# A mixture-of-experts kernel whose ScalarE and VectorE keep the order of the program in the experts, with two more result buffers and one load buffer fewer

## The chip, the cores and the metric

The kernel runs on one core of a Trainium2 chip. The metric is the time of one execution in device microseconds. A core has five engines that run side by side and wait for each other through semaphores: TensorE (PE, matrix products into the accumulator memory PSUM), VectorE (DVE), ScalarE (ACT), GpSimd (POOL) and SyncE (SP, which issues the loads here). Each engine works through its own queue in order, so an instruction that waits holds all those behind it on that engine.

## The reference

Two layers on 256 tokens of 1,024 channels, all in float32. Each layer has a mixer (dilated attention, stick-breaking attention and a convolution, gated and added). The first layer then has a dense feed-forward block, the second a mixture of eight experts, of which each token takes two:

```python
logits = h @ w_router + b_router
top_logits, top_idx = lax.top_k(logits, 2)
gates = softmax(top_logits)
...
def expert_block(xb, e):
    a = xb @ w_exp_gate[e]
    u = xb @ w_exp_up[e]
    return (silu(a) * u) @ w_exp_down[e]
...
x = x + segment_sum(expert_block(...) * gate, token)
```

Each expert has three matrices of 1,024 x 2,816. They have to be loaded in full, whatever the number of tokens.

## The kernel before, in words

**Products.** A float32 weight is split into a high part `hi` (a rounding copy, by ScalarE) and a low part `lo = weight - hi` (a subtraction, by VectorE); both go through TensorE as its fast 32-bit type. `_Stream` does this for all weights: `_make` (line 265) loads a chunk into a `raw` buffer by SyncE's queue, issues `hi` (line 284) and `lo` (line 288) into `part` buffers, and `next` hands the oldest pair out and calls for further ones, up to `AHEAD_E`, that is three units of 128 x 2,048 beyond the one in use. There are `RAW_BUFS + MORE_BUFS` = 9 `raw` buffers in the experts, and 8 `part` buffers, which hold four pairs. A unit of half the size, both parts in one buffer, is called `hilo`.

**An expert** (`expert`, from line 1155) goes through 22 units of gate and up weights, alternately two for the gate (`eg`) and two for the up projection (`eu`), 512 output columns each; the last two units hold 256 columns of both. Such a group of four I call a round. Twelve units (two of them half) of down weights follow (`ed`, two banks in turn). TensorE's products of a unit are in `products` (line 1168). A long expert has up to 128 rows and takes three products per weight tile (`hi` twice, `lo` once), so 12 matmuls per unit. A short expert (at most 64 rows) puts both parts of the activations side by side in the 128 columns of its left operand, and takes two, 8 per unit; the lower half of the result must then be folded onto the upper, for which ScalarE copies it to `low` (line 1180) and TensorE multiplies that by `fold` (line 1183). ScalarE applies Silu into `ea` (line 1210), VectorE multiplies by `eu` (line 1213), TensorE transposes the product (`eaT`, line 1194), and ScalarE and VectorE split the transposed result into `ehl` in a result buffer (`split_evac`, lines 509 and 510). Result buffers come from the function `T`, which takes `MOE_SLABS` = 8 of them in turn in the experts.

**A seam.** At an expert's end both banks of `ed` are split into `yhi` (ScalarE, line 509) and `ylo` (VectorE, line 510), each half of the columns by itself. `scatter` (line 1134) multiplies them by the permutation `pmt` that puts rows back to their tokens (`sc`, lines 1138 and 1139, two banks for each half), ScalarE copies a bank out, scaled by the gate (`add`, line 1143), and GpSimd adds it to `x` (line 1144). In the last expert VectorE does both at once (line 1146). The program asks for all that while the next expert's first units are already under way: `later(n, f)` runs `f` after `n` further units. Odd experts also gather the rows of the next two (`gather`: `pm`, `xg`). `count` ranks the experts by their number of tokens, in E0, and `ranked` in its result is what SyncE reads to address the loads of the third to the eighth expert.

**Order.** The code is written in one order, and a scheduler of the framework decides in which order each engine's queue gets its instructions, from its own estimate of when each could start. What is wrapped in `keep_in_program_order` (`_InOrder`, and the names `act_`, `dve_`) stays in the order written. In the experts, before the change, ScalarE and VectorE instructions are free. The ranks are worked in the order 0, 1, 5, 2, 6, 3, 4, 7; ranks 5, 6 and 7 are short. I call the eight E0 to E7 in the order of work: E2, E4 and E7 are short.

Of the kernel before, what the change touches and what calls it, by code (L numbers as in the profile page):

```python
# [7 lines left out]
F32 = mybir.dt.float32  # L8
# [4 lines left out]
ALU = mybir.AluOpType  # L13
# [20 lines left out]
RAW_BUFS = 5  # L34
PART_BUFS = 4
SLABS = 17
MORE_BUFS = 4
MORE_PARTS = 4
AHEAD = 3 * 1024
AHEAD_E = 3 * 2048  # L40
WARM = 7
MOE_SLABS = 8
UNIT_E = 2048
SHORT = P // 2

# [164 lines left out]
class _InOrder:  # L210


    def __init__(self, tc, engine):
        self.tc = tc
        self.engine = engine
# [7 lines left out]
class _Stream:  # L223
# [3 lines left out]
    def __init__(self, tc, raw_pool, part_pool, ahead):  # L227
        self.tc = tc
        self.nc = tc.nc
        self.raw_pool = raw_pool  # L230
        self.part_pool = part_pool
        self.ahead = ahead
        self.plan = []
        self.units = []
        self.raws = {}
        self.more_pool = None
        self.more_parts = None
        self.hold = None
        self.lo_late = None
        self.turn = -1  # L240
        self.part_turn = -1
        self.made = 0
        self.waiting = 0

    def raw_tile(self, shape):

        n = RAW_BUFS + (MORE_BUFS if self.more_pool else 0)
        self.turn = (self.turn + 1) % n
        pool = self.raw_pool if self.turn < RAW_BUFS else self.more_pool
        return pool.tile(shape, F32, tag="raw", name="raw")  # L250
# [16 lines left out]
    def _make(self):  # L267
        nc = self.nc
        key, ci, u, ku, n = self.units[self.made]
        size = ku * n  # L270
        self.made += 1
        self.waiting += size
        src, length = self.plan[ci]
        if ci not in self.raws:
            raw = self.raw_tile([P, length])
            nc.sync.dma_start(raw, src() if callable(src) else src)
            self.raws = {ci: raw}
        part = self.raws[ci][:, u * size:(u + 1) * size]
        if 2 * size <= UNIT_E:
            both = self.part_tile("hilo")  # L280
            hi, lo = both[:, :size], both[:, size:2 * size]
        else:
            hi, lo = (self.part_tile(q)[:, :size] for q in ("hi", "lo"))
        ins = nc.scalar.activation(hi, part, AF.Copy)  # L284
        if self.lo_late is not None:
            self.tc.keep_in_program_order(ins)
        if self.lo_late is None:
            nc.vector.tensor_tensor(lo, part, hi.bitcast(F32), op=ALU.subtract)  # L288
        else:
            self.lo_late.append(lambda e: e.tensor_tensor(lo, part, hi.bitcast(F32), op=ALU.subtract))  # L290
        return (key, size, hi.rearrange("p (k n) -> p k n", n=n), lo.rearrange("p (k n) -> p k n", n=n))
# [34 lines left out]
def tile_kernel(ctx, tc, x, weights, experts, columns, consts, gains, out, dbg=None):  # L326
    nc = tc.nc
    dbg = dbg or {}
    pe, act, dve, pool = nc.tensor, nc.scalar, nc.vector, nc.gpsimd

    pe_, act_, dve_, pool_ = (_InOrder(tc, e) for e in (pe, act, dve, pool))
# [5 lines left out]
    small = ctx.enter_context(tc.tile_pool(name="small", bufs=4))  # L337
    slab = ctx.enter_context(tc.tile_pool(name="slab", bufs=MOE_SLABS))
    dense = ExitStack()
    slab2 = dense.enter_context(tc.tile_pool(name="slab2", bufs=SLABS - MOE_SLABS))  # L340
    slabs = {"turn": -1, "of": [slab if i < MOE_SLABS else slab2 for i in range(SLABS)]}
    work = dense.enter_context(tc.tile_pool(name="work", bufs=2))
# [57 lines left out]
    ws = _Stream(tc, raw_pool, part_pool, ahead=AHEAD)  # L400
# [633 lines left out]
        rt["slots"].append(sl)  # L1034

    def moe():
        hhi, hlo, rs2, sels, picks, slots = (rt[k] for k in ("hi", "lo", "rs2", "sels", "picks", "slots"))

        low_1 = lambda e: low(1)
# [289 lines left out]
    def to_moe():  # L1329
# [6 lines left out]
        nc.sync.dma_start(rt["gain"], gains)  # L1336
        ws.more_pool = ctx.enter_context(tc.tile_pool(name="more", bufs=MORE_BUFS))
        ws.more_parts = ctx.enter_context(tc.tile_pool(name="more_parts", bufs=MORE_PARTS))
# [10 lines left out]
    for l in range(L):  # L1349
        mixer(l, *[route] * (l == L - 1))  # L1350
        for t in range(TT):
            dump(f"xm{l}{t}", xs[t])
        if l == 0:
            ffn()
            for t in range(TT):
                dump(f"xf{t}", xs[t])
        else:
            moe()
# [37 lines left out]
```

## Time and profile before

| | |
|---|---|
| median of three runs | 1552.11 us (1551.28 to 1553.24) |
| the profiled execution | 1555.26 us |
| its span (first to last instruction) | 1553.4 us |
| TensorE busy | 1469.4 us, 95%, 6717 matmuls |
| VectorE busy | 1197.7 us, 77%, 1261 instructions |
| ScalarE busy | 1009.9 us, 65%, 1056 instructions |
| GpSimd busy | 101.3 us, 7% |
| read from memory | 397.88 MB, 257 GB/s over the span |
| chain that ended last | TensorE 66%, VectorE 18%, ScalarE 8%, "issue" 5% |

The experts fill the second half of the span, from about 751 us on; the rest are the two mixers and the dense block. The table says that TensorE is busy nearly always, but it is an average over stages, and a busy matmul may still be one that was stretched. Where a stage has room is seen from the busy time of each engine in its own stretch; why, from the chain of waits in it. "Idle before" a group of instructions is the time in which the engine had nothing to do ahead of them, with the instruction that ended it. PEclk, the seventh figure of a stretch, is the clock that TensorE was granted, as a share of the full one.

### The profile page before, as it was taken

To read this page: it belongs to the slowest core of one execution; us is meant where nothing else is said; L and a number is where in the kernel's file an instruction comes from. 1 tells how busy PE (TensorE), PEld (TensorE's weight loads), DVE (VectorE), ACT (ScalarE), POOL (GpSimd) and SP (SyncE) were. 2 spreads that over 40 slices of the span, in tenths; PEclk is the share of its full clock that TensorE was granted. 3 is DMA by queue.
4 is the path that set the end of the run, shared out by engine and by line. 5 is a ranking of instruction groups with operands and counts; after the bars stand their busy time and mean duration, and the time that the engine had idled before them with its cause. 6 is when DMAs were issued, how large, how long until landed. Compare 5 with 4: busy or idle time off the path is not lost.

```text
span 1553.4 us, 18165 instructions
## 1 busy us (share of the span) xinstructions
PE 1469.4 (95%) x6717; PEld 1147.1 (74%) x6717; DVE 1197.7 (77%) x1261; ACT 1009.9 (65%) x1056; POOL 101.3 (7%) x69
## 2 busy tenths in 40 slices
PE   9979999999999989999999999889998899999886
PEld 7867787788888777787888887557775577877554
DVE  6898657555547797666898888888888888888777
ACT  6646653544436556663877778777777767766774
POOL 0200000000000200000000202020020010200200
PEclk9999999999999999999899999999999999999998
DMA  8443345555555343447599989999898898988982
GB/s 350 139 168 128 136 162 174 179 189 173 182 189 188 136 163 111 156 167 284 217 374 374 358 324 364 344 349 349 312 395 337 341 358 323 393 327 319 343 328 104
DMA packets 57696, 400.18 MB, mean 258 GB/s; under 512 B 6528, under 2 KB 6784, under 8 KB 10752
## 3 DMA queue, kind: packets, MB, share of 16 engines
q1 hardware_dynamic: 57312, 398.85, 69.3%
q8 instruction: 54, 0.88, 0.2%
q14 instruction: 42, 0.34, 0.1%
q10 hardware_dynamic: 288, 0.10, 0.0%
HBM read 397.88 MB, written 1.05 MB: 257 GB/s over the span
## 4 chain that ended last, share of the span: by engine, by line
PE 66%; DVE 18%; ACT 8%; issue 5%; POOL 2%; DMA 0%; ACTq 0%; DVEq 0%; SPq 0%
PE ed L1168 11%; PE eg L1168 10%; PE eu L1168 9%; DVE lo L288 8%; ACT hi L284 6%; DVE acc L607 4%; DVE hilo L288 3%; PE gt L449 2%; PE gt L447 2%; PE gt L448 2%; POOL qkss L669 1%; PE fg L448 1%; PE fg L449 1%; PE fg L447 1%; PE fd L447 1%
## 5 line engine op out<-in xcount | busy, mean ns | idle before, releaser
L288 DVE TENSOR_TENSOR lo<-raw,hi 128x2048 fp32r<-128x2048 f32 x253 | 586.9, 2338 | 96.1 <-ACT hi L284 94.6
L284 ACT ACTIVATE hi<-raw 128x2048 fp32r<-128x2048 f32 x253 | 477.0, 1913 | 35.5 <-PE ed L1168 18.6
L288 DVE TENSOR_TENSOR hilo<-raw,hilo 128x1024 fp32r<-128x1024 f32 x244 | 295.1, 1221 | 177.4 <-ACT hilo L284 177.1
L284 ACT ACTIVATE hilo<-raw 128x1024 fp32r<-128x1024 f32 x248 | 257.8, 1058 | 230.5 <-PE fd L449 35.5
L1168 PE MATMUL eg<-hi,xg 128*128 128x512 f32 x608 | 160.8, 400 | 2.5 <-ACT hi L284 2.3
L1168 PE MATMUL eu<-hi,xg 128*128 128x512 f32 x520 | 135.3, 397 | 1.8 <-ACT hi L284 1.8
L1168 PE MATMUL ed<-hi,ehl 128*128 128x512 f32 x516 | 134.4, 397 | 1.4 <-ACT hi L284 1.4
L1168 PEld LDWEIGHTS eg<-hi,xg 128*128 128x128 f32 x608 | 110.9, 188 | 32.5 <-ACT hi L284 8.9
L1168 PE MATMUL eg<-lo,xg 128*128 128x512 f32 x376 | 106.1, 403 | 13.4 <-DVE lo L288 13.4
L1168 PEld LDWEIGHTS eu<-hi,xg 128*128 128x128 f32 x520 | 96.9, 189 | 28.5 <-ACT hi L284 6.1
L1168 PEld LDWEIGHTS ed<-hi,ehl 128*128 128x128 f32 x516 | 95.4, 189 | 25.1 <-ACT hi L284 4.3
L1144 POOL TENSOR_TENSOR x<-x,add 128x512 f32<-128x512 f32 x28 | 69.6, 2513 | 640.7 <-ACT add L1143 640.7
L1168 PE MATMUL eu<-lo,xg 128*128 128x512 f32 x320 | 92.1, 409 | 16.3 <-DVE lo L288 16.2
L1168 PE MATMUL ed<-lo,ehl 128*128 128x512 f32 x316 | 89.8, 406 | 13.4 <-DVE lo L288 12.6
L607 DVE SCALAR_TENSOR_TENSOR acc<-uT,cols,acc 128x255 f32<-128x255 f32 (+29 forms) x240 | 97.1, 462 | 0.0
L1168 PEld LDWEIGHTS eg<-lo,xg 128*128 128x128 f32 x376 | 67.9, 188 | 34.3 <-DVE lo L288 20.4
L1168 PEld LDWEIGHTS eu<-lo,xg 128*128 128x128 f32 x320 | 56.7, 188 | 42.4 <-DVE lo L288 29.6
L1168 PEld LDWEIGHTS ed<-lo,ehl 128*128 128x128 f32 x316 | 57.5, 189 | 35.9 <-DVE lo L288 24.0
L447 PE MATMUL gt<-hilo,hhi 128*128 128x512 f32 x192 | 76.9, 401 | 0.0
L449 PE MATMUL gt<-hilo,hhi 128*128 128x512 f32 x192 | 75.1, 391 | 0.0
L448 PE MATMUL gt<-hilo,hlo 128*128 128x512 f32 x192 | 75.1, 391 | 0.0
L509 ACT ACTIVATE ehl<-eaT 128x512 fp32r<-128x512 f32 (+2 forms) x48 | 23.4, 487 | 71.9 <-PE eaT L1194 61.7
(299 smaller groups left out, 2340.4 us busy)
## 6 DMA issues: line engine op xcount, KB each, us to landing
raw<-in_experts_dram SPq DMA_DIRECT2D x255, 1024.0 KB, 6.7
raw<-in_weights_dram SPq DMA_DIRECT2D x111, 1024.0 KB, 4.8
raw<-in_experts_dram SPq DMA_DIRECT2D x18, 512.0 KB, 4.5
raw<-in_weights_dram SPq DMA_DIRECT2D x4, 512.0 KB, 6.8
x<-in_x_dram SPq DMA_DIRECT2D x2, 512.0 KB, 4.3
out_dram<-x SPq DMA_DIRECT2D x4, 256.0 KB, 2.7
gain<-in_gains_dram SPq DMA_DIRECT2D x1, 512.0 KB, 3.5
att<-in_consts_dram SPq DMA_DIRECT2D x1, 448.0 KB, 7.0
```

What stands on the lines that cost most here:

```text
L284: ins = nc.scalar.activation(hi, part, AF.Copy)
L288: nc.vector.tensor_tensor(lo, part, hi.bitcast(F32), op=ALU.subtract)
L447: pe.matmul(dst, ahi, whi, start=first, stop=False)
L448: pe.matmul(dst, alo, whi, start=False, stop=False)
L449: pe.matmul(dst, ahi, wlo, start=False, stop=last)
L509: act.activation(hi, src, AF.Copy)
L607: dve.scalar_tensor_tensor(acc[:, c, lag:], uT[:, c, :S - lag], w, acc[:, c, lag:], op0=ALU.mult, op1=ALU.add)
L669: pool.tensor_tensor(ssf, ssf, half[:, :TT * 8], op=ALU.pow)
L1144: pool.tensor_tensor(xs[t][:, sl], xs[t][:, sl], add, op=ALU.add)
L1168: pe.matmul(b, lhs(q, k0 + j), w[:, j, :], start=k0 + j == 0 and x == 0, stop=k0 + j == nk - 1 and x == len(todo) - 1)
```

## The change

`moe` now replaces the names `act` and `dve` by the wrapped ones and sets a flag in the stream, so that all ScalarE and VectorE instructions of the experts, `hi` and `lo` among them, stay in the order in which the program issues them. TensorE, GpSimd and SyncE are still ordered by the scheduler. Two more of the 17 result buffers are kept for the experts (`MOE_SLABS` 10), and there is one `raw` buffer fewer (8). In the dense part no instruction of ScalarE or VectorE changes its place.

```diff
-MORE_BUFS = 4
+MORE_BUFS = 3
...
-MOE_SLABS = 8
+MOE_SLABS = 10
...
+        self.in_order = False
...
         ins = nc.scalar.activation(hi, part, AF.Copy)
-        if self.lo_late is not None:
+        if self.lo_late is not None or self.in_order:
             self.tc.keep_in_program_order(ins)
         if self.lo_late is None:
-            nc.vector.tensor_tensor(lo, part, hi.bitcast(F32), op=ALU.subtract)
+            ins = nc.vector.tensor_tensor(lo, part, hi.bitcast(F32), op=ALU.subtract)
+            if self.in_order:
+                self.tc.keep_in_program_order(ins)
...
     def moe():
+        nonlocal act, dve
+        act, dve, ws.in_order = act_, dve_, True
```

Three places show how the orders move. In the changed kernel an instruction that goes through the wrapper has the wrapper's line, L219, and those of `_make` are five lines further down or less.

ScalarE in the middle of the short expert E4, a little over a round (`low_9048` is the copy of the same two units in both), before:

```order
L1180 ACTIVATE low_9048<-eg_9017 64x512
L284 ACTIVATE hi_9022<-raw_9020 128x2048
L1210 ACTIVATE ea_9018<-eg_9017,rss_8725 64x512
L284 ACTIVATE hi_9036<-raw_9034 128x2048
L1180 ACTIVATE low_9088<-eu_9019 64x512
L284 ACTIVATE hi_9054<-raw_9052 128x2048
L284 ACTIVATE hi_9076<-raw_9074 128x2048
L509 ACTIVATE ehl_9146<-eaT_9141 128x4x64
L1180 ACTIVATE low_9123<-eg_9092 64x512
```

With the change:

```order
L219 ACTIVATE low_9048<-eg_9017 64x512
L285 ACTIVATE hi_9054<-raw_9052 128x2048
L219 ACTIVATE ehl_9071<-eaT_9066 128x4x64
L285 ACTIVATE hi_9076<-raw_9074 128x2048
L219 ACTIVATE low_9088<-eu_9019 64x512
L219 ACTIVATE ea_9018<-eg_9017,rss_8725 64x512
L285 ACTIVATE hi_9097<-raw_9095 128x2048
L285 ACTIVATE hi_9111<-raw_9109 128x2048
L219 ACTIVATE low_9123<-eg_9092 64x512
L285 ACTIVATE hi_9129<-raw_9127 128x2048
```

Before, a round reads `low`, `hi`, `ea`, `hi`, `low`, `hi`, `hi`, `ehl`; with the change `low`, `hi`, `ehl`, `hi`, `low`, `ea`, `hi`, `hi`. Behind `low_9048` stood `hi_9022`; now it is `hi_9054`, two units further on.

ScalarE at the seam from E2 (short) to E3 (long), from the first `yhi` on before, and from the fourth `hi` of E3 on with the change (`hi_8017`, `hi_8031`, `hi_8049`, `hi_8062` are E3's first four units; `ed_7870`, `ed_7893` E2's two banks; `sc_8080` to `sc_8118` their four products with the permutation):

```order
L509 ACTIVATE yhi_7868<-ed_7870 128x512
L284 ACTIVATE hi_8017<-raw_8005 128x2048
L1143 ACTIVATE add_8083<-sc_8080,gr0_5977 128x512
L1143 ACTIVATE add_8089<-sc_8086,gr1_5983 128x512
L509 ACTIVATE yhi_7868<-ed_7893 128x512
L284 ACTIVATE hi_8031<-raw_8029 128x2048
L1143 ACTIVATE add_8115<-sc_8112,gr0_5977 128x512
L1143 ACTIVATE add_8121<-sc_8118,gr1_5983 128x512
L284 ACTIVATE hi_8049<-raw_8047 128x2048
L1210 ACTIVATE ea_8058<-eg_8057,rss_7312 128x512
L284 ACTIVATE hi_8062<-raw_8060 128x2048
L284 ACTIVATE hi_8094<-raw_8092 128x2048
```

With the change:

```order
L285 ACTIVATE hi_8062<-raw_8060 128x2048
L219 ACTIVATE yhi_7868<-ed_7870 128x512
L219 ACTIVATE add_8083<-sc_8080,gr0_5977 128x512
L219 ACTIVATE add_8089<-sc_8086,gr1_5983 128x512
L285 ACTIVATE hi_8094<-raw_8092 128x2048
L219 ACTIVATE yhi_7868<-ed_7893 128x512
L219 ACTIVATE add_8115<-sc_8112,gr0_5977 128x512
L219 ACTIVATE add_8121<-sc_8118,gr1_5983 128x512
L219 ACTIVATE ea_8058<-eg_8057,rss_7312 128x512
L285 ACTIVATE hi_8127<-raw_8125 128x2048
```

Before, the first `yhi` stands ahead of all `hi` of E3, and each further pair of results has `hi` between. Now the first four `hi` of E3 stand ahead of it, and the fifth, `hi_8094`, behind the first two `add`, the sixth, `hi_8127`, behind the other `yhi`, two further `add` and a Silu.

TensorE at the same seam, from the first `sc` on before, and from the fourth unit of E3 on with the change:

```order
L1138 MATMUL sc_8080<-yhi_7868,pmt_7307 128x512
L1138 MATMUL sc_8086<-yhi_7868,pmt_7307 128x512
L1139 MATMUL sc_8080<-ylo_7869,pmt_7307 128x512
L1139 MATMUL sc_8086<-ylo_7869,pmt_7307 128x512
L1168 MATMUL eg_8057<-hi_8017,xg_7174 128x512 x2
L1168 MATMUL eg_8057<-hi_8017,xg_7206 128x512 x2
L1168 MATMUL eg_8057<-hi_8017,xg_7174 128x512 x2
L1168 MATMUL eg_8057<-hi_8017,xg_7206 128x512 x2
L1138 MATMUL sc_8112<-yhi_7868,pmt_7307 128x512
L1138 MATMUL sc_8118<-yhi_7868,pmt_7307 128x512
```

With the change:

```order
L1173 MATMUL eu_8059<-hi_8062,xg_7237 128x512 x2
L1143 MATMUL sc_8080<-yhi_7868,pmt_7307 128x512
L1143 MATMUL sc_8086<-yhi_7868,pmt_7307 128x512
L1173 MATMUL eu_8059<-hi_8062,xg_7268 128x512 x2
L1173 MATMUL eu_8059<-hi_8062,xg_7237 128x512 x2
L1173 MATMUL eu_8059<-hi_8062,xg_7268 128x512 x2
L1173 MATMUL eu_8059<-lo_8063,xg_7237 128x512 x2
L1173 MATMUL eu_8059<-lo_8063,xg_7268 128x512
L1144 MATMUL sc_8080<-ylo_7869,pmt_7307 128x512
L1144 MATMUL sc_8086<-ylo_7869,pmt_7307 128x512
```

Before, the first `sc` come ahead of E3's first unit (`hi_8017`). With the change they stand in E3's fourth (`hi_8062`, `lo_8063`), three units later.

## Rows read from the trace of the kernel before

**Rows 1.** Busy by stretch, E1 to E7: length, PE, PEld, DVE, ACT, POOL, clock, DMA, GB/s

```profile
848.60:948.80 100.20, 100.20 (x467) 82.24 (x466) 85.48 (x55) 75.83 (x63) 10.36 (x4) 1.00 0.92 347
948.80:1040.10 91.30, 79.77 (x310) 52.26 (x308) 78.18 (x47) 72.56 (x63) 9.14 (x4) 1.00 0.90 345
1040.10:1144.90 104.80, 102.29 (x462) 80.53 (x463) 91.69 (x56) 78.28 (x64) 10.66 (x4) 1.00 0.94 355
1144.90:1239.00 94.10, 80.42 (x311) 52.24 (x309) 77.09 (x48) 73.32 (x62) 8.99 (x4) 1.00 0.90 342
1239.00:1343.30 104.30, 101.81 (x462) 80.34 (x463) 90.72 (x52) 78.21 (x64) 10.67 (x4) 1.00 0.94 356
1343.30:1441.80 98.50, 97.62 (x431) 78.01 (x429) 79.41 (x47) 67.13 (x51) 9.13 (x4) 1.00 0.90 338
1441.80:1553.40 111.60, 85.25 (x309) 53.97 (x309) 87.39 (x54) 75.89 (x64) 10.66 (x4) 0.95 0.68 251
```

**Rows 2.** Chain of waits, middle of E2: start, length, what

```profile
987.97 2.30 DVE lo L288
...
990.32 1.21 PE eu L1168 x4
...
992.23 1.92 ACT hi L284
...
994.17 2.30 DVE lo L288
```

**Rows 3.** Groups by line and shape, ScalarE, the experts: xcount | busy, mean | idle, releasers

```profile
L284 ACT ACTIVATE hi<-raw 128x2048 fp32r<-128x2048 f32 x253 | 477.0, 1913 | 35.5 <-PE ed L1168 18.6 <-PE eg L1168 9.3 <-PE eu L1168 5.6
...
L1143 ACT ACTIVATE add<-sc,gr 128x512 f32<-128x512 f32 x20 | 13.0, 686 | 3.6 <-PE sc L1139 3.1 <-POOL x L1144 0.5
...
L1180 ACT ACTIVATE low<-eg 64x512 fp32r<-64x512 f32 x18 | 10.7, 595 | 21.8 <-PE eg L1168 21.7
L1210 ACT ACTIVATE ea<-eg,rss 64x512 f32<-64x512 f32 x15 | 10.2, 683 | 0.3
L509 ACT ACTIVATE yhi<-ed 128x512 fp32r<-128x512 f32 x16 | 9.4, 596 | 27.3 <-PE ed L1168 27.3
...
L509 ACT ACTIVATE ehl<-eaT 128x256 fp32r<-128x256 f32 x20 | 7.6, 382 | 10.3 <-PE eaT L1194 5.6 <-PE ed L1168 4.4
```

**Rows 4.** The same groups, VectorE, the experts

```profile
L288 DVE TENSOR_TENSOR lo<-raw,hi 128x2048 fp32r<-128x2048 f32 x253 | 586.9, 2338 | 96.1 <-ACT hi L284 94.6 <-PE eu L1168 0.8
```

**Rows 5.** VectorE in order of time, start of E2 and late E7

```profile
963.27 5.02 DVE L288 TENSOR_TENSOR lo<-raw,hi 128x2048 fp32r<-128x2048 f32 x2 [1.74 <-ACT hi L284]
...
1508.74 4.49 DVE L288 TENSOR_TENSOR lo<-raw,hi 128x2048 fp32r<-128x2048 f32 x2 [0.53 <-ACT hi L284]
```

**Rows 6.** TensorE in order of time, middle of E1: start, length, what

```profile
878.97 2.03 PE L1168 MATMUL eu<-hi,xg 128*128 128x512 f32 x8
...
881.77 2.03 PE L1168 MATMUL eu<-hi,xg 128*128 128x512 f32 x8
```

**Rows 7.** TensorE in order of time, middle of E4

```profile
1181.69 0.46 PE L1194 MATMUL eaT<-con,ea 64*128 64x64 f32 x4
```

**Rows 8.** Busy time by stretch: E3 from end of `ed`; end of E7

```profile
1038.50:1066.90 28.40, 26.36 (x109) 19.30 (x110) 23.97 (x13) 22.69 (x18) 10.66 (x4) 1.00 0.96 374
1507.30:1543.60 36.30, 29.39 (x110) 19.92 (x109) 30.71 (x22) 23.84 (x19) 0.00 (x0) 0.95 0.44 164
```

**Rows 9.** Operations of tile `raw`, 1325 to 1345 us: its loads

```profile
DMA to landing us min/median/max: 7.6/9.0/10.3
```

**Rows 10.** TensorE in order of time, start of E7

```profile
1448.71 1.39 PE L1168 MATMUL eg<-lo,xg 128*128 128x512 f32 x4 [1.96 <-DVE lo L288]
```

**Rows 11.** Busy time by stretch, start of E7

```profile
1446.00:1450.00 4.00, 2.04 (x9) 1.34 (x8) 3.60 (x2) 2.86 (x3) 4.00 (x3) 0.94 0.77 252
1450.00:1454.00 4.00, 4.00 (x12) 2.49 (x11) 3.25 (x2) 3.81 (x4) 3.08 (x1) 0.63 0.81 295
```

**Rows 12.** Chain of waits, start of E7

```profile
1445.26 3.41 DVE lo L288
```

## The prediction, made before the changed kernel was run

> **What bounds the kernel now.** I read the busy time expert by expert first [rows 1]. The experts E0 to E7 come in the order of `RANKS`; E2, E4 and E7 are short (8 matmuls per unit), the others long (12). In a long expert TensorE is the limit: E1 is busy for all of its 100.20 us, E6 for 97.62 of 98.50. In the short ones it isn't: E2, E4 and E7 leave TensorE idle for 11.5, 13.7 and 26.4 us, and neither VectorE nor ScalarE is full there. E3 and E5 each last 4 to 5 us longer than E1, with the same work. So order can win only in the three short experts and at the seams.
>
> The chain of waits in the middle of E2 [rows 2] says why a short expert is slow: a `lo` (2.30), four matmuls (1.21), then, past a `low`, the next `hi` (1.92), then a `lo` again: 6.2 us per two units, 12.4 per round of four (one `eg`, one `eu`). ScalarE's order has the `hi` of a unit only behind a `low` which waits for products, so it runs hardly ahead. Loads don't come into it: of ScalarE's idle time ahead of `hi`, 33.5 of 35.5 us is put down to TensorE [rows 3].
>
> Prices: `hi` 1.91, `ea` .68, `low` .60, `ehl` .38, `add` .69, `yhi` .60 [rows 3]; on VectorE a `lo` has a mean of 2.34, stretched ones with it [rows 4], and back to back two take 4.49 [rows 5], 2.2 to 2.25 each. VectorE's own parts of `ea` and `ehl` I take as long as ScalarE's. A long unit takes TensorE 881.77 − 878.97 = 2.80 us [rows 6], so .23 per matmul and 1.87 per short unit; four transposes take .46 [rows 7].
>
> **Step 1, rounds of a short expert.** In the new order `ehl` stands between two `hi`, and ScalarE blocks there until TensorE has turned `ea`. From the end of the `lo` ahead of that: matmuls and transposes some 1.5 (with waits between), `ehl` .38, `hi` 1.91, `low` .60, `ea` .68, `hi` 1.91: 7.0. Two `lo` follow, 4.4: a round of 11.4 in place of 12.4. Units 8 to 20 are three rounds: −3.0 in each short expert. Behind the blocked `ehl` stand two `hi`, behind these VectorE's `lo`, and behind `lo` SyncE's next load. Bounds: nothing, if the block lasts 1 us longer; and a round of 10.1, if it never binds and VectorE sets the pace (four `lo` 9.0, `ea` .7, `ehl` .4), so −6.9. I take the middle one, since the order names the wait.
>
> **Step 2, seams into a short expert.** Four `hi` of the next expert now run ahead of `yhi`, but `add`, `add` stand ahead of the fifth `hi`, and `yhi`, `add`, `add` ahead of the sixth; an `add` waits for the `sc` matmuls, which TensorE's order has one unit or more into the expert, and ScalarE does nothing else meanwhile. E1 to E2, from the first `eg`: fourth `hi` 1.9 (its buffers come free then), `yhi` 2.5, unit 1 and the `ylo` half of `sc` 5.4, two `add` 6.7, fifth `hi` 8.6, `low`, `yhi` 9.8; `lo` of unit 4 10.9, `ylo` 11.6, `sc` 12.1, two `add` 13.5, sixth `hi` 15.4, seventh 17.3, `low`, `ea`, eighth 20.5, two `lo`: unit 8 is split at 25.0. Before it was split at 963.27 + 5.02 = 968.29 [rows 5], 19.5 after 948.8. So +5.5, −3.0 for step 1, −1.0 for the `ed` units (a third of step 4's 2.9): **E2 +1.5**. E4 would then be as long as E2, 92.8 against 94.1 [rows 1]: **E4 −1.3**.
>
> E6 to E7 has the `sc` only in unit 3. The same sum gives 8.2 for the first `add`, 11.4 fifth `hi`, 14.9 second pair of `add`, 18.1 sixth `hi`, 23.2 eighth, 27.7 for unit 8. Before: the tail begins at 1507.3, at the end of unit 20 [rows 8], less three rounds of 12.4 is 1470.1, or 28.3; and the four `sc` ahead of the first `eg` (.9) move into the expert. So −1.5, then −3.0: see step 4.
>
> **Step 3, seams into a long expert.** From the end of `ed`: four units and four `sc` are 12.1; then two `add` and `hi` make TensorE wait 3.1; `yhi`, `lo`, `ylo`, `sc`, two `add`, `ea`, `hi` make it wait 3.3 more before unit 5. Eight units, eight `sc` and four transposes (24.7) become 31.0, against 28.4 now [rows 8]. The rest now takes 78.0 in E3 (1066.9 to 1144.9) and 77.5 in E5; at E1's pace it takes 100.2 − 24.7 = 75.5. **E3 +.1, E5 +.6.** E0 to E1 loses nothing now and would wait about 1.9 ahead of unit 5, up to 3.6 with late `lo`: I take **E1 +2.5**. In E5 to E6 TensorE has `sc` one unit earlier, the fifth `hi` is ready at 8.6 and nothing waits: **E6 −.9**, the idle time that it has.
>
> **Step 4, E7's end.** From 1507.3 to 1543.6 VectorE is busy 30.71 of 36.30 us [rows 8]; 5.6 are waits. In the new order those left are .4 and .9 (step 1), .3, and 1.1 for the `hi` behind the last `ehl`, which pays back the wait at `yhi`: 33.4. So −2.9, and **E7 −7.4** in all.
>
> **Step 5, what costs nothing.** A load has eight units, not nine, to land and be used: 8 × 2.8 = 22.4 us, less some 5 by which `hi` leads `lo`, against 10.3 for the slowest landing where the queue is fullest [rows 9]. If that cover went, one unit (2.8) per stall would show as ScalarE waiting for a DMA. The two added result buffers only let the order run without a deadlock. The block of router operations (`count`) in E0 and SyncE's `ranked` loads, now together, stand beside E0's full TensorE: 0, at worst 3. The dense layers keep their order: 0.
>
> **Step 6, the clock.** At E7's start TensorE waited 1.96 us for a `lo` [rows 10]; after a stretch of 4 us with 2.04 busy the granted clock was .94, then .63, and 12 matmuls filled 4.00 us that hold 17 at .23 [rows 11]: a loss near 1.5 us, part of a stretch at the lower of two levels (1.2 against 2.4 GHz). Step 3's stalls are longer than that one. Bounds for E3 and E5 are 0 (E2 to E3 now, shorter stalls, no dip) and 3.0 each; their nearest row is E7's: I take 1.5 each, **+3.0**. In the short experts TensorE has slack, and E7's present dip is in its 28.3.
>
> The Trainium skill ("TensorE: Matmul & The Clock Gate", Why this matters for your kernels) says to leave no idle gaps between bursts of matmuls, since the clock halves after them. It speaks against this change; the dip at E7's start agrees, and the third rival is what the rule would do at every seam.
>
> **Sum.** 2.5 + 1.5 + .1 − 1.3 + .6 − .9 − 7.4 + 3.0 = −1.9 us. The profiled execution of 1555.26 would become 1553.4; it stands 3.15 above the median of the runs, 1552.11, which becomes **1550.2**. A measurement here can tell about 0.2%, 3.1 us, from nothing.
>
> **Rivals.** (1) My forecast: gains in E7, costs at the seams, nearly cancelled. Its own range comes from the seams, some 1 us either way at each of five. Chance .50: .18 faster, .26 same, .06 slower.
>
> (2) ScalarE's blocks don't bind: `eaT` comes early, and VectorE sets a round of 10.1. Then 3 × 3 × 1.3 = 11.7 more is won: −13.6, **1538.5**. For it: VectorE and ScalarE have room in E2, 78.18 and 72.56 busy of 91.30 us [rows 1], and ScalarE's order now reaches two units further ahead. Against it: the order has one `ehl` per round behind products. With it goes the case that the order's gain is larger at the seams than I see, since E3 and E5 lose over 4 us each now. Chance .22, faster.
>
> (3) The seams: each of the five slow ones (E2, E3, E4, E5, E7) blocks ScalarE twice, the clock dips at the second block too (+1.5 each, +7.5), and a `lo` on the chain meets the GpSimd add, which stretches it to 3.41 [rows 12] (+1.1 each, +5.5): +11.1, **1563.2**. It decides from the point at which a slow seam costs 1.0 more than I reckon (1.9 and the 3.1 that can be told, over five). For it: rows 10 to 12 show all of it at one seam. Against it: E2 to E3 stalls twice now without a dip. Chance .26, slower.
>
> (4) The change does little: TensorE's and the scheduler's order binds anyway, and rounds stay 12.4 while the seams, whose four early `hi` pay for the late two, even out: 1552. Chance .02, same.
>
> So faster .40, same .28, slower .32. The range goes from 1537 to 1566, a unit or so beyond rivals 2 and 3; the forecast's own is 1545 to 1556.
>
> **What would show it.** Right: rounds of 11.4 in E4, ScalarE's idle ahead of `ehl` and `add` up, ahead of `low` down; the wait in front of units 4 and 5 of E3 near 3 us each; E7 7 us shorter, E1 2 longer. Wrong: rounds at 10.3 (rival 2), granted clock under 1 at four seams or more (rival 3), ScalarE waiting for DMA ahead of `hi` (step 5).

## The result, and the profile after

The changed kernel takes 1571.66 us (median of 4 runs, 1570.20 to 1572.10), the kernel before beside it 1552.67: a ratio of 1.0117 [1.0099, 1.0136]. It is slower by 1.2%, 5.7 us beyond the range that I gave. The profiled execution has a span of 1570.2 us, 16.8 more than before.

Busy time by stretch of the changed kernel, one expert per row, E0 to E7 from `eg` to `eg` (columns as in [rows 1]; the first row is E0, whose like before took 97.4 us):

```profile
751.40:850.30 98.90, 96.71 (x442) 78.82 (x441) 89.72 (x86) 74.56 (x57) 0.00 (x0) 1.00 0.91 347
850.30:953.10 102.80, 100.95 (x468) 82.14 (x466) 83.85 (x55) 74.07 (x63) 5.06 (x4) 1.00 0.87 339
953.10:1045.90 92.80, 81.50 (x307) 52.56 (x306) 75.60 (x47) 74.40 (x63) 5.03 (x4) 0.98 0.91 341
1045.90:1157.70 111.80, 105.42 (x467) 85.16 (x466) 89.03 (x57) 75.94 (x64) 4.97 (x4) 0.95 0.87 339
1157.70:1250.80 93.10, 81.88 (x306) 52.49 (x305) 75.56 (x47) 74.38 (x63) 5.03 (x4) 0.98 0.88 337
1250.80:1362.60 111.80, 105.47 (x468) 85.21 (x467) 89.11 (x57) 76.08 (x64) 4.97 (x4) 0.95 0.87 338
1362.60:1458.30 95.70, 95.70 (x428) 77.73 (x426) 81.73 (x49) 70.34 (x53) 5.10 (x4) 1.00 0.90 347
1458.30:1570.20 111.90, 87.85 (x314) 55.83 (x312) 79.59 (x53) 70.97 (x63) 4.97 (x4) 0.92 0.70 260
```

In the kernel before, four `sc` stood ahead of the first `eg` of E3, E5 and E7. So both kernels are compared from the end of the last `ed` of one expert to the end of the last `ed` of the next:

| | E0 | E1 | E2 | E3 | E4 | E5 | E6 | E7 | sum |
|---|---|---|---|---|---|---|---|---|---|
| predicted, with the clock in E3 and E5 | 0 | +2.5 | +1.5 | +1.6 | −1.3 | +2.1 | −.9 | −7.4 | −1.9 |
| measured (.3 ahead of E0 with it) | +1.8 | +2.5 | +3.3 | +5.2 | +1.0 | +5.5 | −1.5 | −1.0 | +16.8 |

Two long experts and the gain that E7 didn't have make up most of the miss. TensorE is busy 105.4 and 105.5 us in E3 and E5, at a mean clock of .95; E1, with as many matmuls (467 to 468 each), takes 101.0 at a clock of 1.00.

The seam from E2 to E3, changed kernel: TensorE in order of time, the rows with the two waits, then ScalarE in the same stretch.

```profile
1060.75 0.97 PE L1173 MATMUL eg<-hi,xg 128*128 128x512 f32 x3 [2.76 <-ACT hi L285]
...
1069.62 3.78 PE L1173 MATMUL eg<-hi,xg 128*128 128x512 f32 x8 [3.32 <-ACT hi L285]
```

```profile
1057.64 1.26 ACT L219 ACTIVATE add<-sc,gr 128x512 f32<-128x512 f32 x2 [8.60 <-PE sc L1144]
1058.79 1.91 ACT L285 ACTIVATE hi<-raw 128x2048 fp32r<-128x2048 f32 x1
1060.59 0.60 ACT L219 ACTIVATE yhi<-ed 128x512 fp32r<-128x512 f32 x1
1065.93 1.26 ACT L219 ACTIVATE add<-sc,gr 128x512 f32<-128x512 f32 x2 [4.74 <-PE sc L1144]
```

ScalarE stands 8.60 us and then 4.74 us in front of an `add`; the next `hi` is queued behind it and runs as soon as the two `add` (the second time a Silu too) are done, and TensorE waits for it 2.76 and 3.32 us. What this does to the clock is in the stretches of 4 us (columns as in [rows 11]):

```profile
1054.00:1058.00 4.00, 3.99 (x18) 2.99 (x16) 0.65 (x2) 0.36 (x1) 0.00 (x0) 1.00 1.02 426
1058.00:1062.00 4.00, 1.25 (x5) 1.00 (x6) 1.27 (x1) 3.19 (x4) 2.49 (x2) 0.96 1.00 416
1062.00:1066.00 4.00, 4.00 (x13) 3.07 (x11) 1.64 (x2) 0.07 (x1) 0.00 (x0) 0.61 0.79 289
1066.00:1070.00 4.00, 0.68 (x3) 0.38 (x2) 0.40 (x1) 4.00 (x5) 2.49 (x2) 0.82 0.36 143
1070.00:1074.00 4.00, 4.00 (x10) 3.14 (x10) 4.00 (x2) 3.17 (x2) 0.00 (x0) 0.50 0.20 41
1074.00:1078.00 4.00, 4.00 (x17) 3.18 (x16) 2.96 (x3) 0.00 (x0) 0.00 (x0) 0.83 1.00 410
```

Behind each wait the granted clock falls: to .61 in one stretch, then to .50, the lower of the two levels (1.2 and 2.4 GHz), where ten matmuls fill 4.00 us.

Rounds of a short expert, E4 of the changed kernel: VectorE in order of time, then ScalarE's row of the wait.

```profile
1196.91 0.41 DVE L219 TENSOR_TENSOR ehl<-eaT,ehl 128x256 fp32r<-128x256 f32 x1
1198.10 2.29 DVE L289 TENSOR_TENSOR lo<-raw,hi 128x2048 fp32r<-128x2048 f32 x1 [0.78 <-ACT hi L285]
1201.23 4.50 DVE L289 TENSOR_TENSOR lo<-raw,hi 128x2048 fp32r<-128x2048 f32 x2 [0.83 <-ACT hi L285]
1205.64 0.73 DVE L219 SCALAR_TENSOR_TENSOR ea<-eu,rss,ea 64x512 f32<-64x512 f32 x1
1206.30 2.27 DVE L289 TENSOR_TENSOR lo<-raw,hi 128x2048 fp32r<-128x2048 f32 x1
1208.50 0.41 DVE L219 TENSOR_TENSOR ehl<-eaT,ehl 128x256 fp32r<-128x256 f32 x1
```

```profile
1207.46 0.38 ACT L219 ACTIVATE ehl<-eaT 128x256 fp32r<-128x256 f32 x1 [1.90 <-PE eaT L1199]
```

From `ehl` to `ehl` is 11.59 us; the prediction had 11.4. The `ea` of VectorE (its multiply with `eu`) comes as the fourth of the round's six; TensorE can turn it only then, ScalarE stands 1.90 us in front of `ehl`, and the two `hi` behind make VectorE wait .78 and .83.

Three groups by line and shape, changed kernel:

```profile
L289 DVE TENSOR_TENSOR lo<-raw,hi 128x2048 fp32r<-128x2048 f32 x253 | 572.9, 2289 | 133.9 <-ACT hi L285 132.0
L285 ACT ACTIVATE hi<-raw 128x2048 fp32r<-128x2048 f32 x253 | 474.4, 1916 | 16.2 <-PE ed L1173 15.8
...
L1149 POOL TENSOR_TENSOR x<-x,add 128x512 f32<-128x512 f32 x28 | 35.1, 1276 | 699.3 <-ACT add L219 699.3
```

VectorE's idle time ahead of `lo` is up from 96.1 to 133.9 us [rows 4]; ahead of `hi` nothing is put down to a DMA, as step 5 had it.

### The profile page after: what moved, and what is told of

It reads as the page before. It is cut to its first block, busy times and chain, and to the rows that moved or that the text cites. A ratio compares the mean times of both kernels' runs of the same rounds, so it can differ in the third digit from the quotient of the medians.

```text
span 1570.2 us, 18159 instructions
## 1 busy us (share of the span) xinstructions
PE 1481.4 (94%) x6717; PEld 1159.3 (74%) x6717; DVE 1183.3 (75%) x1261; ACT 1003.8 (64%) x1056; POOL 67.2 (4%) x69
## 4 chain that ended last, share of the span: by engine, by line
PE 70%; DVE 15%; ACT 9%; issue 4%; POOL 1%; DMA 0%; ACTq 0%; DVEq 0%; SPq 0%
PE eg L1173 13%; PE ed L1173 11%; PE eu L1173 10%; ACT hi L285 6%; DVE lo L289 4%; DVE acc L610 4%; DVE hilo L289 3%; PE gt L452 2%; PE gt L450 2%; PE gt L451 2%; POOL qkss L672 1%; PE fg L451 1%; PE fg L452 1%; PE fg L450 1%; PE fd L452 1%
## 5 line engine op out<-in xcount | busy, mean ns | idle before, releaser
L289 DVE TENSOR_TENSOR lo<-raw,hi 128x2048 fp32r<-128x2048 f32 x253 | 572.9, 2289 | 133.9 <-ACT hi L285 132.0
L1173 PE MATMUL eg<-hi,xg 128*128 128x512 f32 x608 | 169.7, 412 | 27.8 <-ACT hi L285 27.8
L1173 PEld LDWEIGHTS eg<-hi,xg 128*128 128x128 f32 x608 | 115.1, 194 | 62.9 <-ACT hi L285 34.4
L1173 PE MATMUL eu<-hi,xg 128*128 128x512 f32 x520 | 145.4, 407 | 1.9 <-ACT hi L285 1.9
L219 ACT ACTIVATE ehl<-eaT 128x512 fp32r<-128x512 f32 (+2 forms) x48 | 23.5, 489 | 124.6 <-PE eaT L1199 124.6
L1173 PE MATMUL ed<-lo,ehl 128*128 128x512 f32 x316 | 90.6, 404 | 11.6 <-DVE lo L289 11.1
L1173 PEld LDWEIGHTS eg<-lo,xg 128*128 128x128 f32 x376 | 72.7, 198 | 26.6 <-DVE lo L289 10.9
L1149 POOL TENSOR_TENSOR x<-x,add 128x512 f32<-128x512 f32 x28 | 35.1, 1276 | 699.3 <-ACT add L219 699.3
```

The lines of the kernel that those rows point to most:

```text
L219: return self.tc.keep_in_program_order(getattr(self.engine, name)(*args, **kw))
L289: ins = nc.vector.tensor_tensor(lo, part, hi.bitcast(F32), op=ALU.subtract)
L1149: pool.tensor_tensor(xs[t][:, sl], xs[t][:, sl], add, op=ALU.add)
L1173: pe.matmul(b, lhs(q, k0 + j), w[:, j, :], start=k0 + j == 0 and x == 0, stop=k0 + j == nk - 1 and x == len(todo) - 1)
```

## The experiments

Three theories stood at first: the loss is ScalarE's order, with its waits at the seams (A in the expectations), or it is the buffers (B), or VectorE's order (C). VectorE's place for `ea` (D), against that of its other operations (E), came out of the first four runs. "Free" below means that the scheduler places the operation, as in the kernel before.

**e1, the buffers alone**, on the kernel before:

```
-MORE_BUFS = 4
+MORE_BUFS = 3
...
-MOE_SLABS = 8
+MOE_SLABS = 10
```

> The kernel before with 10 result and 8 load buffers, its order free. If the loss is one of order at the seams (theory A): the same as before, 1550 to 1555 us, each expert within 1 us of before. If the missing load buffer costs the time (theory B): 1560 to 1572, and ScalarE's idle time ahead of hi is put down to DMA.

1557.12 us, 1.0026 [1.0016, 1.0036]. Between the two: 3.7 us, in the profile at E1 (+1.2) and E2 (+3.6), less .9 in E0 and .7 in E7, and not in E3 or E5 (104.8 and 104.4, as before). The scheduler also places other rows differently with these rings, so it isn't certain that the buffers themselves cost that. Most of the result's 19 us is not theirs.

**e2, the seams free**: the changed kernel, with `yhi`, `ylo` and `add` left to the scheduler.

```
+        free_act, free_dve = act, dve
         act, dve, ws.in_order = act_, dve_, True
...
-                split_evac(yhi[:, sl], ylo[:, sl], bank)
+                free_act.activation(yhi[:, sl], bank, AF.Copy)
+                free_dve.tensor_tensor(ylo[:, sl], bank, yhi[:, sl].bitcast(F32), op=ALU.subtract)
...
-                    act.activation(add, b, AF.Copy, scale=g)
+                    free_act.activation(add, b, AF.Copy, scale=g)
```

> The changed kernel, but yhi, ylo and add are left to the scheduler; all else of ScalarE and VectorE keeps the program's order. Theory A (ScalarE blocked at add, two TensorE stalls of 3 us per seam, and the clock dips behind them): E3 and E5 fall from 111.8 to 104 to 107 us, E1 back to about 100, the whole to 1548 to 1558. Theory B (load buffers) or theory C (VectorE's order, or rounds): 1565 or more, E3 and E5 still over 110.

1548.82 us, .9972 [.9961, .9982]: 22.8 less than with the whole change. E3 and E5 fall from 111.9 and 111.8 to 106.9 us each, measured as in the table above (105.1 and 105.0 from the first `eg`); E1 falls to 101.9 only. The order at the seams (of `ylo`, an operation of VectorE, with it) is by itself enough to turn a slower kernel into one that is no slower than before.

**e3, ScalarE's order alone** (VectorE free, `lo` too; the diff), and **e4, VectorE's alone** (ScalarE and `hi` free, in the same way):

```
-            if self.in_order:
-                self.tc.keep_in_program_order(ins)
...
-        nonlocal act, dve
-        act, dve, ws.in_order = act_, dve_, True
+        nonlocal act
+        act, ws.in_order = act_, True
```

> Only ScalarE keeps the program's order; VectorE is free. Theory A: as the changed kernel, 1567 to 1574, with the same stalls of about 3 us ahead of units 4 and 5 of E3. Theory C (VectorE's order costs the time): near before, 1550 to 1557.

> Only VectorE keeps the program's order; ScalarE is free, so yhi, add and hi stand as the scheduler puts them. Theory A: near before, 1548 to 1558, no stall over 1.5 us ahead of unit 4 of E3. Theory C: 1565 or more.

e3 takes 1537.22 us, .9901 [.9885, .9918], and contradicts A as I had put it: with all of ScalarE's blocks in place, at the seams too, the kernel is faster than before, and faster than C had it. e4 takes 1556.42, 1.0025 [1.0014, 1.0037]: beside e1, which has the same buffers, VectorE's order by itself costs nothing, but where ScalarE keeps the order too it costs 34.4 us (1571.66 against e3). It takes both, as in the rounds above: the late `ea` costs time because ScalarE stands in front of `ehl` with two `hi` behind it. Busy time by stretch of e3, E2, E3 and E7:

```profile
945.80:1031.70 85.90, 79.01 (x307) 51.34 (x306) 74.97 (x47) 74.39 (x63) 5.02 (x4) 1.00 0.93 369
1031.70:1142.10 110.40, 104.98 (x467) 85.33 (x466) 88.20 (x57) 76.04 (x64) 4.98 (x4) 0.95 0.88 340
...
1432.90:1535.00 102.10, 83.97 (x314) 55.05 (x312) 79.59 (x53) 71.00 (x63) 4.98 (x4) 0.95 0.73 287
```

E2 and E7 are 6.9 and 9.8 us shorter (E4, at 86.1, is 7.0) than with the whole change; E3 stays long, at a clock of .95. So, with ScalarE in order, the short experts lose by VectorE's order, and the seams by ScalarE's.

**e5, the multiply alone free**, everything else in order as changed:

```
-                    dve.scalar_tensor_tensor(a[rows], bu[rows, :n], r1(), a[rows], op0=ALU.mult, op1=ALU.mult)
+                    free_dve.scalar_tensor_tensor(a[rows], bu[rows, :n], r1(), a[rows], op0=ALU.mult, op1=ALU.mult)
```

> The changed kernel, but VectorE's ea (the product with eu) alone is left to the scheduler, which puts it two lo earlier in a round. Theory D (ScalarE blocks at ehl until ea, behind two more lo on VectorE, is turned): E2 and E4 fall from 93 to 86 to 87 us and E7 from 112 to 102 to 104, as with ScalarE's order alone; E0 stays at 99; 1538 to 1546 in all. Theory E (it is the order of lo, ehl or ylo on VectorE): over 1560.

1543.44 us, .9940 [.9919, .9960]: one kind of operation brings back 28.2 of the 34.4 us that a free VectorE does. E2, E4 and E7 take 86.1, 85.9 and 104.5 us, 21.3 less together. E3 and E5 fall too, to 106.4 and 109.2, though ScalarE's seams are as in the changed kernel. Both still have the first wait, of 2.76 and 2.75 us; the second is 2.32. The stretch right behind the first wait, in E3 and then in E5:

```profile
1055.00:1059.00 4.00, 2.99 (x13) 1.98 (x11) 1.88 (x2) 1.38 (x3) 0.61 (x1) 1.00 0.95 350
1247.00:1251.00 4.00, 4.00 (x12) 3.17 (x11) 2.25 (x2) 0.00 (x0) 0.00 (x0) 0.57 0.92 326
```

The clock stays at 1.00 in E3 and falls to .57 in E5, and E3's first eight units take 30.6 us, E5's 33.4. So a wait of that length lowers the clock in one seam and not in another of the same execution, and some 3 of the 29 us that this execution gains are of that kind. Why is open.

**e6, with `count`'s VectorE operations free too** (`dve` to `free_dve` in `count`):

> As e5_ea_free, and the VectorE operations of count in E0 are free as well. Theory D with the router block as the cause of E0's loss: E0 falls from 99 to 96.5 us, and the whole is 2 to 3 us below e5_ea_free, at 1535.5 to 1540. If E0's loss is of another operation's order: the same as e5_ea_free.

1541.78 us, .9925 [.9909, .9942]: the two intervals overlap, and it is a miss: E0 goes from 101.3 to 98.4 in the profiles and not to the 96.4 of e3. `count` may be part of what E0 loses; that isn't shown, and the rest I haven't found.

**e7, ScalarE in order, its seams and VectorE free** (e2 and e3 in one):

> ScalarE alone in the program's order (as e3_scalar_only), with yhi and add left to the scheduler. If ScalarE's blocks at add cost E3 and E5 their time (theory A): E3 and E5 fall from 110 to 105 us, E2 and E4 stay at 84 to 87, 1525 to 1531 in all. If the four early hi of a seam are what makes the short experts faster (rival): E2, E4 and E7 lose what E3 and E5 gain, 1534 to 1540.

1514.41 us, .9750 [.9734, .9767]: the best kernel here, 2.5% faster than before, and 11 us below the range that I expected if A held. The four kernels make a square: changed 1571.7, seams free 1548.8, VectorE free 1537.2, both 1514.4. Freeing the seams brings 22.8 with VectorE in order and 22.8 with it free; freeing VectorE 34.4 and 34.4. So the two add up. That they do to .1 us is luck: the runs of the changed kernel spread over 1.9 us, those of e2 over 4.6. VectorE in e7, middle of E4:

```profile
1156.74 0.41 DVE L511 TENSOR_TENSOR ehl<-eaT,ehl 128x256 fp32r<-128x256 f32 x1
1157.07 2.27 DVE L289 TENSOR_TENSOR lo<-raw,hi 128x2048 fp32r<-128x2048 f32 x1
1159.27 0.74 DVE L1217 SCALAR_TENSOR_TENSOR ea<-eu,rss,ea 64x512 f32<-64x512 f32 x1
1159.93 6.68 DVE L289 TENSOR_TENSOR lo<-raw,hi 128x2048 fp32r<-128x2048 f32 x3
1166.54 0.41 DVE L511 TENSOR_TENSOR ehl<-eaT,ehl 128x256 fp32r<-128x256 f32 x1
```

`ea` comes two `lo` earlier, `eaT` is there before ScalarE asks, VectorE has no gap left, and a round takes 9.80 us. E2 and E3 of e7:

```profile
948.90:1031.40 82.50, 78.70 (x311) 52.22 (x309) 75.00 (x48) 72.95 (x62) 8.61 (x4) 1.00 0.98 396
1031.40:1133.10 101.70, 100.16 (x462) 81.39 (x463) 90.41 (x56) 78.68 (x64) 10.67 (x4) 1.00 0.94 360
```

**e8, e7 with the old buffers** (eight for results, nine for loads):

> As e7_scalar_seam_free, with the buffers of the kernel before (8 for results, 9 for loads). If the buffers are needed only for VectorE's program order: the same as e7, 1510 to 1518. If ScalarE's order alone also wants ten result buffers (ehl waits for a free one, the ring closes up): E2, E4 and E7 rise by 3 us or more each, 1524 or more. A ninth load buffer gains nothing either way, since no ScalarE wait is put down to a load.

1527.21 us, .9823 [.9809, .9836]. ScalarE's waits for others in e8 (total, times, longest) have a row that e7 lacks:

```profile
ACT ehl L219 <- PE ed L1172: 32.9, 5, 10.5
```

`ehl` waits there for the `ed` that read its buffer: no result buffer is free. E0 and E6 take 104.9 and 104.4 us, against 96.7 and 97.9 in e7. I had looked for it in the short experts. Once ScalarE keeps the order, the old buffers cost 12.8 us; in step 5 I gave the added ones no time at all.

**e9, the program's own order with `ea` earlier**, both engines in order, seams free:

```
-                            later(3, folded)
+                            later(1, folded)
...
-                    later(1, lambda: turn(c0, a))
+                    later(3 if short and c0 < 2560 else 1, lambda: turn(c0, a))
```

> The changed kernel with seams free (as e2_seam_free) and VectorE in the program's order, but the program itself has ea two units earlier in the short experts: the fold one unit after its products in place of three, the transposes three units later in place of one, so that three lo stand between ea and ehl in place of one. Theory D (the distance from ea to ehl on VectorE closes the ring, not the keeping of an order as such): E2 and E4 fall from 90 to 82 to 84 us, E0 stays at 99, 1516 to 1524. If keeping VectorE's order costs by something else: 1540 or more, as e2.

1568.46 us, 1.0090 [1.0072, 1.0108], a miss. `folded` also holds the Silu of ScalarE, which I moved with it:

```profile
ACT ea L219 <- PE eg L1189: 55.8, 16, 4.1
```

ScalarE now stands in front of the Silu for the folding matmul, 55.8 us in all.

**e10, only the fold of `e_u` earlier**: as e9, with `later(1 if key == "e_u" else 3, folded)`.

> As e9_program_ea_early, but Silu stays where the changed kernel has it: only the fold of eu comes one unit after its products, so that VectorE's ea alone moves two units up in the program, and three lo stand between it and ehl. ScalarE's order in a round is that of e7_scalar_seam_free. Theory D (what closes the ring is how late the producer stands ahead of the instruction that waits for it): E2 and E4 at 82 to 84 us, E0 at 99, 1515 to 1522 in all. If keeping VectorE's order costs by itself, whatever the order: 1540 or more.

1520.91 us, .9791 [.9774, .9809]. E2 and E4 take 80.9 and 81.0 us, shorter than in e7, with both engines in program order; E2:

```profile
952.20:1033.10 80.90, 78.34 (x310) 52.38 (x308) 75.83 (x47) 72.14 (x62) 6.21 (x4) 1.00 1.00 399
```

So keeping the order costs nothing in the rounds by itself; that order's place for `ea` does.

**e11, the waits filled**: the changed kernel, order kept, with matmuls of zero weights in the two waits of E3 and of E5.

```
+            units = [0, None]
...
                         whi, wlo = ws.next(key)
+                        for x in range({4: 10, 5: 12}.get(units[0], 0) if fill else 0):
+                            pe.matmul(b, fold[:SHORT], units[1][:SHORT, 0, :], start=k == 0 and x == 0, stop=k == 0 and x == 9)
+                        units[0] += 1
+                        units[1] = whi
                         products(b, whi, wlo, lambda q, k: part(i, q, k), k, KT)
...
+                             if p % 2 and p + 1 < NE else lambda: None, fill=p in (3, 5))
```

> The changed kernel with its order kept, and 22 matmuls of zero weights added in E3 and in E5: ten ahead of the fifth unit and twelve ahead of the sixth, in the two waits of 2.76 and 3.32 us that the seam leaves there. They add zeros to the sum of the unit that follows; nothing else on any engine moves. If the lower clock behind the waits is what makes E3 and E5 hold 5 us more of TensorE's work than E1 does (105.4 against 100.2 us): the granted clock stays at 1.00 through both seams, E3 and E5 fall from 111.9 and 111.8 to 106.5 to 108.5, and the kernel takes 1561 to 1566. If the clock costs nothing, because the matmuls behind the waits wait for ScalarE and VectorE anyhow: E3 and E5 stay within 1 us of 111.8, and the kernel takes 1570 to 1573. If the added matmuls outlast the waits, it is slower than that by up to 1 us per expert.

1563.77 us, 1.0071 [1.0057, 1.0086]: 7.9 less than the changed kernel. E3 and E5 take 107.8 and 107.7 us, 4.0 and 4.1 less (the profiled execution, the shortest of its six, is 11.1 shorter: 3.0 of that are in E2, E4 and E7, where nothing was added). TensorE at the second wait, and the stretches that answer to those above:

```profile
1064.07 3.04 PE L1183 MATMUL eg<-hi,fold 64*128 64x512 f32 x12
1067.47 2.12 PE L1174 MATMUL eg<-hi,xg 128*128 128x512 f32 x8 [0.36 <-ACT hi L285]
```

```profile
1062.00:1066.00 4.00, 4.00 (x17) 2.83 (x17) 1.03 (x2) 2.23 (x4) 1.46 (x2) 1.00 0.93 326
1066.00:1070.00 4.00, 3.64 (x16) 2.60 (x15) 2.55 (x2) 4.00 (x3) 1.07 (x1) 1.00 0.20 82
1070.00:1074.00 4.00, 4.00 (x21) 3.29 (x20) 4.00 (x3) 1.25 (x2) 0.00 (x0) 1.00 0.76 274
```

The `hi` still come late: between the program's own matmuls the two gaps are 2.75 and 3.33 us. But the clock stays at 1.00, and the eight matmuls behind the second gap take 2.12 us in place of 3.78. The first eight units of E3, from the end of `ed`, take 31.1 us where the changed kernel takes 35.2. The waits are the same, the clock is not: in these executions it costs 4.1 us per long seam.

## Why the prediction was wrong

**What bounds the kernel**: right in the main. The time moved in the short experts and at the seams, but for E0, and for the rest of E3 and E5 (below).

**Step 1, rounds, and step 2, seams into a short expert: their sum right to .1 us in E2, by luck, and a little low in E7.** VectorE's rows in E2, where unit 8 ends at 972.61 + 4.50 and unit 20 at 1007.86 + 4.50 = 1012.36:

```profile
972.61 4.50 DVE L289 TENSOR_TENSOR lo<-raw,hi 128x2048 fp32r<-128x2048 f32 x2 [0.42 <-ACT hi L285]
...
1007.86 4.50 DVE L289 TENSOR_TENSOR lo<-raw,hi 128x2048 fp32r<-128x2048 f32 x2 [0.84 <-ACT hi L285]
```

Unit 8 is split 24.0 us after the first `eg` (I had 25.0), unit 20 at 59.3 (I had 59.2): the seam was 1.0 shorter than I had it, and the three rounds, 12.2, 11.5 and 11.5, were 1.1 longer than 34.2. In E7 unit 8 comes at 28.6 instead of 27.7, and a round takes 11.6. The middle one of my three bounds was the right one, for the reason given: ScalarE blocks at `ehl`.

**Step 3, the waits at the seams: right.** 2.76 and 3.32 us for 3.1 and 3.3; the eight units that I put at 31.0 take 31.1 in e11, at full clock; E1 +2.5 for +2.5. E6 gained 1.5 for .9. What I let E3 and E5 gain behind the seam, by running on at E1's 75.5, came only in part: 76.7 and 76.5.

**Step 4, the end of a short expert: wrong by 8.6 us.** I let the waits of E7's end shrink from 5.6 to 2.7 us, since most seemed to go with the old order, and gave E2 and E4 a third of it. They stayed: VectorE's rows behind unit 20's `lo` in E7, those with a wait:

```profile
1525.94 2.29 DVE L289 TENSOR_TENSOR lo<-raw,hi 128x2048 fp32r<-128x2048 f32 x1 [1.02 <-ACT hi L285]
1529.07 4.49 DVE L289 TENSOR_TENSOR lo<-raw,hi 128x2048 fp32r<-128x2048 f32 x2 [0.84 <-ACT hi L285]
...
1537.77 2.29 DVE L289 TENSOR_TENSOR lo<-raw,hi 128x2048 fp32r<-128x2048 f32 x1 [1.02 <-ACT hi L285]
...
1543.49 8.90 DVE L289 TENSOR_TENSOR lo<-raw,hi 128x2048 fp32r<-128x2048 f32 x4 [1.51 <-ACT hi L285]
...
1553.85 1.41 DVE L219 SCALAR_TENSOR_TENSOR x<-sc,gr,x 128x512 f32<-128x512 f32 x2 [0.85 <-PE sc L1144]
```

They come to 5.2 us, and all but the last are the `hi` that are late behind a block at `ehl`, as in the rounds. The stretch from the end of unit 20's `lo` (1521.73) to that of the last `hilo` (1558.66) took 36.9 us, not 33.4: 2.5 of the 3.5 are waits, and the rest an `ea` and an `ehl` (1.1) that stood ahead of unit 20 before and stand behind it now, which I hadn't counted. What follows took 11.5 in place of 9.8, and the clock falls there too:

```profile
1556.00:1560.00 4.00, 3.56 (x9) 2.77 (x10) 2.66 (x3) 0.00 (x0) 0.00 (x0) 0.58 0.22 83
```

In e11, where nothing was added in E7, the clock is 1.00 through the last ten `ed` and the same end takes 9.9, so that part differs between executions. In E2 and in E4, from unit 20 to the end of `ed`, it is 33.7 us; I had 32.0. e5 shows whose wait this is: with `ea` alone free, the stretch that took 36.9 us takes 33.1, with 2.4 of waits.

**Step 6, the clock: the right mechanism, its size too small by 5.2 us.** I took 1.5 us for each of E3 and E5 from the one dip in the trace of before, with 3.0 as the upper bound. There are two dips per seam, the second all the way down, and e11 prices them at 4.1 us: 8.2 in place of 3.0. I should have priced the clock at each wait that step 3 had found. The Trainium skill ("TensorE: Matmul & The Clock Gate", Why this matters for your kernels) advises against idle gaps between bursts of matmuls, for the clock falls behind them. The trace of the changed kernel agrees, at .61 and .50; in e5 one such gap, of 2.76 us in E3, leaves the clock at 1.00.

**Step 5, what costs nothing: nearly.** Loads don't show, as said. E0 lost 1.5 us where I had 0 and at worst 3; e4, with VectorE's order alone, has an E0 of 99.0 us and e3, without it, 96.4, so it is VectorE's order. The added result buffers do more than prevent a deadlock: e8 prices them, with the load buffer given for them, at 12.8 us.

**The rivals.** The third was nearest: slower, by the seams. Its clock at the second block is what happened, and so did its sign: the clock falls at all five slow seams, in E2 to .57, in E4 to .61 and in E7 to .66 and .57 (stretches of about 4 us) besides E3 and E5. What it costs in the short experts no run shows. The other half of that rival did not happen: `lo` isn't stretched by GpSimd's add (mean 2289 ns, against 2338 [rows 4]), and GpSimd's own add is short (1276 ns): ScalarE's block leaves VectorE idle during most of GpSimd's adds. The second, with VectorE setting a round of 10.1, isn't what the change does, but e7 does it, at 9.80.

The miss is 18.7 us: step 6 5.2; step 4 8.6, in E7 5.2 (3.5, and 1.7 at its very end) and in E2 and E4 1.7 each; E0 1.8; the other 3.1 are 1.0 and .8 in E3 and E5, 1.5 in E7's seam and rounds, .1 and .4 in those of E2 and E4, less .6 in E6 and .1 of rounding.

What stays open: why a free VectorE gives E3 and E5 another 3.4 us (105.1 in e2, 101.7 in e7), the rest of E0's loss, e1's 3.7 us, and why the clock stays up in E3 of e5.

## What to carry to other kernels

In an engine kept in program order, each wait holds up all that the program put behind it, so the program must issue each operation where its input is really there: here one multiply that stood two `lo` too late cost 28 us, and the evacuations at the seams 23, while ScalarE's order in the rest of the experts, with the buffers for it, won 39 (1553.4 to 1514.4). So apply such an order to the steady loop, leave the rare operations between two stages to the scheduler, and give it the buffers that it asks for. Where a change adds waits to TensorE, price behind each one the slower matmuls as well as the wait, as a bound: the clock did not fall behind every one.

## What the runs showed of the hardware

A wait of 2.76 us and one of 3.32, whose ends are 9 us apart, cost 4.1 us beyond themselves by the lower clock in E3 and in E5, and matmuls of zero weights in those waits bring it back. In e5 one seam keeps a clock of 1.00 behind a wait of 2.76 us, and another, behind 2.75, falls to .57. GpSimd's add of 128x512 takes 1276 ns here and took 2513 in the kernel before, by the page of that one:

```profile
L1144 POOL TENSOR_TENSOR x<-x,add 128x512 f32<-128x512 f32 x28 | 69.6, 2513 | 640.7 <-ACT add L1143 640.7
```

The operation is the same; before, VectorE was splitting beside it. Each delays the other: an add beside a `lo` took up to 3.35 us there, and a `lo` 3.41 [rows 12] in place of 2.2; all 19 `lo` of that trace that took over 2.35 us overlap an add. The Trainium skill ("Perfetto Trace Analysis", Tensor Engine Instruction) has ScalarE, VectorE and GpSimd as strict queues, first in, first out. The rows of the seam from E2 to E3 agree: ScalarE idles for 8.60 us in front of an `add` with the next `hi` behind it.
